# The opening stage of a hybrid decoder block: an order written out for four engines, constants loaded later, query and key blocks per pair of token blocks

## The chip, the cores and the metric

The kernel runs on one core of a Trainium2 chip. The metric is the device time of one execution in microseconds, the median of three runs; lower is better. Engines are named as in the profile: PE is TensorE, DVE is VectorE, ACT is ScalarE, POOL is GpSimd, SP is the queue that only issues transfers. ACT issues transfers too (ACTq).

## The reference

One layer of a decoder block on x of 1024 tokens by 1024 channels, in float32. What matters here is its beginning:

```
u = rms_norm(h, mix_pre_g)                       # h = x
z = einsum('bsd,de->bse', u, w_in)               # 1024 -> 4096 columns
p, q, k, v, gate_a, gate_b = split(z)            # 512 each for p, q, k, v; 1024 for each gate
ya = pool_mixer(p, ...) @ w_branch_a             # windows 2, 4, 8, 16; divided by min(t+1, window)
yb = diff_attention(q, k, v, lambda, ...) @ w_branch_b     # 4 heads, each with two softmaxes
m  = sigmoid(gate_a) * ya + sigmoid(gate_b) * yb
h  = h + rms_norm(m @ w_out, mix_post_g)         # then a SwiGLU feed-forward with its own norms
```
lambda comes from four vectors of 64 numbers: exp(sum(lam_q1 * lam_k1)) - exp(sum(lam_q2 * lam_k2)) + 0.2.

## The kernel before

Precision: each float32 operand of a product is held as a high part `hi` (rounded to the matmul format fp32r by an ACT copy) and a low part `lo` (the difference, by a DVE subtraction), and each product is three matmuls, hi·hi, hi·lo and lo·hi, accumulated in PSUM (`mac`, `triple`).

The big products run as Strassen-like units: `seven_steps` forms the products of two column blocks of weights with both halves of the tokens from seven instead of eight quarter products. Its moving operands are the dictionary `U`: A11, A12, A21, A22 (the normed, transposed x: first index is the half of the tokens, 512 each, second the half of the channels) and four sums S1 to S4 of them; its stationary operands `W` are B11, B21, B22 and T1 to T4, made by `weights` from two raw weight blocks. The sums need the whole of x, so they aren't there at first. Therefore the query and key blocks of heads 0 and 1 (`firsts`, four features of 128 columns) are computed directly from A11 to A22 by `common`, while x still comes in, and the first unit (head 2) starts with line 232 when they are done.

The opening stage, lines 285 to 429, handles x in eight blocks of 128 tokens (`tb`). For each block: load (`load_x`, L304), sum of squares on ACT (`square`, L129), mean on DVE (L124) and its power -1/2 on POOL (L125), scaling by that and by the gain vector g1 on DVE (`normed`, L350), eight transposes of 128x128 on PE into one PSUM tile `x_t` of two banks (L381), high parts on ACT (L385), low parts on DVE (L87), both read from PSUM. For the first four blocks a raw copy goes to `traws` by ACT (L401); for the last four ACT copies half of it (L404) and DVE forms the sums from it and from PSUM (L161). There are two such PSUM tiles, so the transposes of a block wait until the block two before has been read by ACT and DVE. The four weight blocks are loaded by `first_raw` (L207), their high parts taken by ACT (L329) and their low parts by POOL, in four parts each (L334).

Head 0's q and k are computed in pairs of token blocks (`first_pair`, 256 columns a matmul) from block 3 on; head 1's q and k come after, with 512 columns a matmul. `qk_done` splits a finished half of q or k into high and low parts (ACT, then DVE) and sends it to DRAM through the ACT queue (L316).

The order of ACT, DVE and POOL within the loop is as written (`tc.manual_schedule`), but instructions from outside the loop may be put between them; the order of PE and of the transfers is the scheduler's. It put the constants' loads (psc, sgc and four lambda vectors, L432 to L436) at the head of the ACT queue, the scaling of sgc (L446) before the first square, the counts for the pooling windows (iota on POOL, minimum and reciprocal on DVE, L448 to L451) before the first norm, and parts of head 2's and head 3's weight sums (`wf_t`, L161) between the blocks' instructions.

Buffers: 16 of kind `a8` (8 KB a partition: U, traws) and 14 of kind `b4` (4 KB: x blocks, g1, first weights, W, `qk_st`); PSUM tiles `mm`, `fil` (one bank) and `pair` (two banks), two of each.

Of the kernel before, what the change touches and what calls it, by code (L numbers as in the profile page):

```python
# [10 lines left out]
F32 = mybir.dt.float32  # L11
F32R = mybir.dt.float32r
AF = mybir.ActivationFunctionType
ALU = mybir.AluOpType
# [25 lines left out]
def block_kernel(ctx, tc, x, w_in, pool_mix, pool_scale, w_branch_a, lam_q1, lam_k1, lam_q2,  # L40
# [78 lines left out]
    cnt = cp.tile([P, 4, 16], F32, name="cnt")  # L119

# [89 lines left out]
    def weights(first, second):  # L210

        W = {}

        def operand(a, *names):
            for _ in weight_operand(W, a, *names):
                pass

        g, u = raw_weights(first, "wraw"), raw_weights(second, "whi")
        operand(g, "B11", "B21")
        t13, t24 = (wp.tile([P, 2, 4, P], F32, tag="wlo", bufs=2, name=name("wf_t")) for _ in range(2))  # L220
        tt(t13[:, 0], u[:, 0], g[:, 0], ALU.subtract)
# [5 lines left out]
        operand(u[:, 1:], "B22")  # L227
        return W

# [77 lines left out]
    def qk_done(h, e, t, src, st=None):  # L307
# [8 lines left out]
        nc.scalar.dma_start(qkd[h][e][:, :, half(t)], f32(st))  # L316
# [14 lines left out]
    def first_lo(i, part):  # L331
        raw, hi, lo = plain[firsts[i]]
        k = slice(2 * part, 2 * part + 2)
        nc.gpsimd.tensor_tensor(out=lo[:, k], in0=raw[:, k], in1=f32(hi[:, k]), op=ALU.subtract)  # L334

    def common(h, e, t, o, c):
# [15 lines left out]
    for tb in range(2):  # L352
        xts.append(load_x(tb))
    nc.sync.dma_start(g1, mix_pre_g.partition_broadcast(P))
    xts.append(load_x(2))
    first_raw(0)
    first_raw(1)
    for tb in range(3, 5):
        xts.append(load_x(tb))
    with tc.manual_schedule(engines={nc.scalar.engine, nc.vector.engine, nc.gpsimd.engine}):  # L360
        for tb in range(2):
            square(tb)
            rstd(tb)
        for tb in range(2):
            normed(tb)
        first_hi(0)
        for part in range(4):
            first_lo(0, part)
        square(2)
        rstd(2)  # L370
        o = [(fil("q"), fil("k")), (mm("q"), mm("k"))]

        def first_pair(i):
            for e in range(2):
                common(0, e, i // 2, o[i // 2][e], slice(i % 2 * 2 * P, (i % 2 + 1) * 2 * P))

        for tb in range(NB):
            t, cols = tb // 4, slice(tb % 4 * P, (tb % 4 + 1) * P)
            both = pair("x_t")
            for k in range(KD):  # L380
                nc.tensor.transpose(both[:, k // 4, k % 4 * P:(k % 4 + 1) * P], xts[tb][:, k * P:(k + 1) * P], ident)  # L381
            v = [both[:, kq, :].rearrange("p (k t) -> p k t", k=4) for kq in range(2)]
            ops = [[a[:, :, cols] for a in U[f"A{t + 1}{kq + 1}"]] for kq in range(2)]
            for kq in range(2):
                nc.scalar.copy(ops[kq][0], v[kq])  # L385
            if tb + 3 < NB:
                square(tb + 3)
            if tb in (0, 2, 4):
                first_hi(tb // 2 + 1)
            for kq in range(2):  # L390
                sub(ops[kq][1], v[kq], ops[kq][0])
            if tb + 2 < NB:
                normed(tb + 2)
            if tb + 3 < NB:
                rstd(tb + 3)
            if tb < 6:
                for part in range(2):
                    first_lo(tb // 2 + 1, part + tb % 2 * 2)
            if t == 0:
                for kq in range(2):  # L400
                    nc.scalar.copy(traws[f"A1{kq + 1}"][:, :, cols], v[kq])  # L401
            else:
                s1, s2, s3, s4 = (traws[f"S{i + 1}"][:, :, cols] for i in range(4))
                nc.scalar.copy(s1, v[0])  # L404
                tt(s1, v[1], s1, ALU.add)
                tt(s2, s1, s2, ALU.subtract)
                tt(s3, v[1], s2, ALU.subtract)
                tt(s4, s4, s2, ALU.subtract)
            if tb + 5 < NB:
                xts.append(load_x(tb + 5))  # L410
            if tb < 2:
                first_raw(tb + 2)
            if tb in (3, 5, 7):
                first_pair(tb // 2 - 1)
            if tb == 7:
                for e in range(2):
                    qk_done(0, e, 0, o[0][e])
    first_pair(3)
    for e in range(2):
        qk_done(0, e, 1, o[1][e])  # L420
    W = weights(w_cols(o_q, 2), w_cols(o_k, 2))
    for t in range(2):
        o = (fil("q"), fil("k")) if t == 0 else (mm("q"), mm("k"))
        for e in range(2):
            common(1, e, t, o[e], slice(0, HALF))
            qk_done(1, e, t, o[e])
    for n in ("S1", "S2", "S3", "S4"):
        U[n] = operand(n)
        split(U[n], traws[n])


    nc.scalar.dma_start(psc, pool_scale.rearrange("(g p) -> p g", p=P))  # L432
    nc.scalar.dma_start(sgc, subln_g.rearrange("(p o) -> p o", o=1))
    lamt = temp("sg").rearrange("p (i d) -> p i d", d=HD)
    for i, t in enumerate(lams):
        nc.scalar.dma_start(lamt[:, i, :], t.partition_broadcast(P))  # L436
    lsum, lexp, nlam = small(2, "lsum"), small(2, "lexp"), cp.tile([P, 1], F32, name="nlam")
    for i in range(2):
        nc.vector.tensor_tensor_reduce(out=lamt[:, 4, :], in0=lamt[:, 2 * i, :], in1=lamt[:, 2 * i + 1, :],
                                       scale=1.0, scalar=0.0, op0=ALU.mult, op1=ALU.add,  # L440
                                       accum_out=lsum[:, i:i + 1])
    nc.scalar.activation(lexp, lsum, AF.Exp)

    nc.vector.tensor_tensor(out=nlam, in0=lexp[:, 1:2], in1=lexp[:, 0:1], op=ALU.subtract)
    nc.vector.tensor_scalar(nlam, nlam, -LAMBDA_INIT, None, op0=ALU.add)
    nc.scalar.mul(sgc, sgc, 1.0 - LAMBDA_INIT)  # L446
    for g, w in enumerate(WINDOWS):
        nc.gpsimd.iota(cnt[:, g, :], pattern=[[1, 16]], base=1, channel_multiplier=0,  # L448
                       allow_small_or_imprecise_dtypes=True)
        nc.vector.tensor_scalar(cnt[:, g, :], cnt[:, g, :], float(w), None, op0=ALU.min)  # L450
    nc.vector.reciprocal(cnt, cnt)  # L451

    later = []

# [710 lines left out]
```

## Time and profile before

| what | value |
|---|---|
| median of three runs | 1292.57 us (1290.82 to 1293.42) |
| the profiled execution | 1293.83 us, of which the span is 1292.0 us |
| mean granted clock of PE in it | 0.995 |
| instructions | 15663 |
| PE busy | 1248.5 us, 97% of the span |
| DVE, ACT, POOL busy | 836.6, 581.8, 139.0 us |
| first transposes of x | start at 12.00 us |
| first matmul of the first query block | 21.38 us |
| first matmul of the first unit (head 2) | 81.48 us |

Times within the profile are counted from the start of the span. In a timeline row the first two numbers are the start and how long the row lasted, `x8` says that eight like instructions in a row are merged, and the bracket gives the engine's idle time before it and what ended it. In a table of groups, "busy, mean ns of one" are followed by idle time and its releasers. Matmuls are pipelined: what one costs in a stream is the distance between two starts, not the duration in its row.

### The profile page before, as it was taken

What the parts mean: (1) busy time and instruction counts of PE and PEld (TensorE: products, weight loads), DVE (VectorE), ACT (ScalarE), POOL (GpSimd) and SP (SyncE); (2) the same over time, 40 slices, a digit from 0 to 9 for tenths busy, and PEclk for the clock granted to TensorE, in tenths of its full rate; (3) what the DMA queues carried; (4) which work ended last, traced back from release to release, by engine and by line L of the source; (5) the groups of instructions that cost most, each with busy time, mean ns of one, the idle gap of its engine ahead of it and who ended that gap; (6) DMA issues with size and microseconds to landing.
All of it is one profiled execution on the core that took longest, in us unless ns stands there. A gap on an engine that the chain in (4) does not pass through costs nothing.

```text
span 1292.0 us, 15663 instructions
## 1 busy us (share of the span) xinstructions
PE 1248.5 (97%) x5856; PEld 1038.3 (80%) x5856; DVE 836.6 (65%) x1303; ACT 581.8 (45%) x1033; POOL 139.0 (11%) x129
## 2 busy tenths in 40 slices
PE   4899999999989999999999999999999999999997
PEld 4788778888778887878878888888888888888886
DVE  4866685454369988655599565565566538865666
ACT  6444335344486666244564333333333334444542
POOL 3100000000101001001102111111110111000221
PEclk9899999999999999999999999999999999999999
DMA  7245246432598421543333323233223258733235
GB/s 248 66 159 183 100 152 197 131 118 86 173 307 221 139 73 43 168 160 131 112 106 114 105 91 101 96 122 123 86 86 114 98 197 307 242 101 91 89 107 203
DMA packets 139788, 179.16 MB, mean 139 GB/s; under 512 B 8000, under 2 KB 94528, under 8 KB 137280
## 3 DMA queue, kind: packets, MB, share of 16 engines
q1 hardware_dynamic: 127776, 146.56, 36.0%
q10 hardware_dynamic: 11936, 31.60, 6.3%
q8 instruction: 46, 0.75, 0.2%
q14 instruction: 30, 0.25, 0.1%
HBM read 124.39 MB, written 53.74 MB: 138 GB/s over the span
## 4 chain that ended last, share of the span: by engine, by line
PE 82%; DVE 7%; ACT 4%; DMA 3%; issue 2%; POOL 1%; ACTq 0%; SPq 0%; DVEq 0%; POOLq 0%
PE Y L232 9%; PE Y L233 9%; PE Y L234 9%; PE X L232 5%; PE X L233 5%; PE X L234 5%; PE Yd L233 3%; PE Yd L234 3%; PE Yd L232 3%; PE Z L233 2%; PE Z L234 2%; PE Z L232 2%; PE wo L818 2%; PE wo L819 2%; PE wo L817 2%
## 5 line engine op out<-in xcount | busy, mean ns | idle before, releaser
L161 DVE TENSOR_TENSOR p<-Z,p 128x512 f32<-128x512 f32 x35 | 24.2, 691 | 158.4 <-PE Z L234 158.4
L233 PE MATMUL Y<-A_lo,Wh 128*128 128x512 f32 x296 | 115.7, 391 | 0.3 <-DVE A_lo L87 0.3
L232 PE MATMUL Y<-A_hi,Wh 128*128 128x512 f32 x296 | 115.3, 390 | 0.0
L234 PE MATMUL Y<-A_hi,Wl 128*128 128x512 f32 x296 | 115.1, 389 | 0.0
L232 PE MATMUL Y<-S_hi,Wh 128*128 128x512 f32 x280 | 109.2, 390 | 0.0
L232 PE MATMUL X<-S_hi,Wh 128*128 128x512 f32 x280 | 109.1, 389 | 0.1
L233 PE MATMUL Y<-S_lo,Wh 128*128 128x512 f32 x280 | 109.1, 390 | 0.0
L234 PE MATMUL Y<-S_hi,Wl 128*128 128x512 f32 x280 | 109.1, 390 | 0.0
L234 PE MATMUL X<-S_hi,Wl 128*128 128x512 f32 x280 | 109.0, 389 | 0.0
L233 PE MATMUL X<-S_lo,Wh 128*128 128x512 f32 x280 | 109.0, 389 | 0.0
L201 ACT CAST Wh<-wf_t 128x1024 fp32r<-128x1024 f32 x70 | 72.8, 1053 | 69.2 <-PE X L233 30.7
L87 DVE TENSOR_TENSOR w_op<-wd,w_op 128x512 fp32r<-128x512 f32 x77 | 56.4, 732 | 55.2 <-ACT w_op L165 55.2
L87 DVE TENSOR_TENSOR Wl<-wf_t,Wh 128x1024 fp32r<-128x1024 f32 x70 | 86.6, 1244 | 4.6 <-ACT Wh L201 4.6
L201 ACT CAST Wh<-w_raw 128x1024 fp32r<-128x1024 f32 x72 | 60.6, 843 | 63.1 <-PE Z L233 41.9
L165 ACT CAST w_op<-wd 128x512 fp32r<-128x512 f32 x77 | 47.9, 622 | 89.1 <-PE Yd L234 34.4
L87 DVE TENSOR_TENSOR Wl<-w_raw,Wh 128x1024 fp32r<-128x1024 f32 x72 | 69.6, 966 | 14.5 <-ACT Wh L201 14.5
L233 PE MATMUL Yd<-w_op,s_op 128*128 128x512 f32 x176 | 68.7, 390 | 0.2 <-DVE w_op L87 0.2
L232 PE MATMUL Yd<-w_op,s_op 128*128 128x512 f32 x176 | 68.6, 390 | 0.0
L234 PE MATMUL Yd<-w_op,s_op 128*128 128x512 f32 x176 | 68.3, 389 | 0.0
L161 DVE TENSOR_TENSOR wf_t<-w_raw,wf_t 128x512 f32<-128x512 f32 x70 | 65.7, 938 | 1.0
L233 PEld LDWEIGHTS Y<-A_lo,Wh 128*128 128x128 f32 x296 | 55.6, 188 | 11.9 <-DVE A_lo L87 0.7
L232 PEld LDWEIGHTS Y<-A_hi,Wh 128*128 128x128 f32 x296 | 55.6, 188 | 11.6
(259 smaller groups left out, 3050.5 us busy)
## 6 DMA issues: line engine op xcount, KB each, us to landing
s_raw<-fsd SPq DMA_DIRECT2D x35, 512.0 KB, 3.7
w_raw<-in_w_in_dram SPq DMA_DIRECT2D x32, 512.0 KB, 4.0
w_raw<-in_w_ffn_gate_dram SPq DMA_DIRECT2D x22, 512.0 KB, 3.6
w_raw<-in_w_ffn_up_dram SPq DMA_DIRECT2D x22, 512.0 KB, 3.7
fsd<-fss SPq DMA_DIRECT2D x11, 1024.0 KB, 3.8
wd<-in_w_ffn_down_dram SPq DMA_DIRECT2D x44, 256.0 KB, 5.1
fsd<-F SPq DMA_DIRECT2D x33, 256.0 KB, 2.2
qkd<-qk_st ACTq DMA_DIRECT2D x16, 512.0 KB, 3.5
```

The costliest lines, as they stand in the source:

```text
L87: nc.vector.tensor_tensor(out=o, in0=a, in1=f32(hi), op=ALU.subtract)
L161: nc.vector.tensor_tensor(out=o, in0=a, in1=b, op=op)
L165: nc.scalar.copy(hi, a)
L201: nc.scalar.copy(hi, a)
L232: nc.tensor.matmul(o, ah, bh, start=start, stop=False, skip_group_check=goes_on)
L233: nc.tensor.matmul(o, ah, bl, start=False, stop=False, skip_group_check=goes_on)
L234: nc.tensor.matmul(o, al, bh, start=False, stop=stop, skip_group_check=goes_on)
L817: nc.tensor.matmul(o[e], mh[:, k, :], wh, start=k == 0, stop=False)
L818: nc.tensor.matmul(o[e], mh[:, k, :], wl, start=False, stop=False)
L819: nc.tensor.matmul(o[e], ml[:, k, :], wh, start=False, stop=k == KD - 1)
```

## The change

All of it is in the opening stage and in what was hoisted into it.

- The order of PE, ACT, DVE and POOL is written out, instruction by instruction, from the first square to the last sum operand; the weight steps for head 2 (`weights_steps`, the old `weights` cut by yields) and the stores of q and k are placed in it. The issue of a store's transfer (`post`) is placed some instructions behind its conversion.
- The loads of x, g1 and the first weights are issued in another order, and the constants' loads and the iota stand after block 7's copies. The exponential, lambda, sgc and counts come after the units of heads 2 and 3.
- All four first features are computed in pairs of token blocks (`feature(f, p)`), 256 columns a matmul; for the first pair all eight hi·hi matmuls come first, then hi·lo, then lo·hi (`by_pass`).
- ACT takes a high part and a raw copy of every block (`take`); low parts from block 2 on (`take_lo`) and the sums (`take_sums`) read the raw copy in SBUF, not PSUM.
- The low parts of the first weights are taken by DVE, one instruction for each block, not by POOL in four.

```diff
@@ weights
-    def weights(first, second):
-        W = {}
+    def weights_steps(W, first, second):
...
         g, u = raw_weights(first, "wraw"), raw_weights(second, "whi")
+        yield
         operand(g, "B11", "B21")
...
+        yield
         operand(t13, "T1", "T3")
...
+        yield
         operand(t24, "T2", "T4")
+        yield
         operand(u[:, 1:], "B22")
@@ qk_done
-        nc.scalar.dma_start(qkd[h][e][:, :, half(t)], f32(st))
+        if post is None:
+            nc.scalar.dma_start(qkd[h][e][:, :, half(t)], f32(st))
+        else:
+            post.append(lambda: nc.scalar.dma_start(qkd[h][e][:, :, half(t)], f32(st)))
@@ first weights
-    def first_lo(i, part):
+    def first_lo(i):
         raw, hi, lo = plain[firsts[i]]
-        k = slice(2 * part, 2 * part + 2)
-        nc.gpsimd.tensor_tensor(out=lo[:, k], in0=raw[:, k], in1=f32(hi[:, k]), op=ALU.subtract)
+        sub(lo, raw, hi)
@@ common
+        if by_pass:
+            for i, (w, a) in enumerate(((hi, 0), (hi, 1), (lo, 0))):
+                for k in range(KD):
+                    nc.tensor.matmul(o[:, c], w[:, k, :], U[f"A{t + 1}{k // 4 + 1}"][a][:, k % 4, c],
+                                     start=i == 0 and k == 0, stop=i == 2 and k == KD - 1)
+            return
@@ loads: before x0 x1 g1 x2 w0 w1 x3 x4, then x5 w2 x6 w3 x7 in the loop
+    xts.append(load_x(0))
+    xts.append(load_x(1))
     nc.sync.dma_start(g1, mix_pre_g.partition_broadcast(P))
+    first_raw(0)
     xts.append(load_x(2))
+    xts.append(load_x(3))
     first_raw(1)
+    first_raw(2)
+    xts.append(load_x(4))
+    first_raw(3)
@@ the steps (the loop over tb, first_pair and what followed up to L451 are taken out)
+    def turn(tb):
+        both = pair("x_t")
+        for k in range(KD):
+            nc.tensor.transpose(both[:, k // 4, k % 4 * P:(k % 4 + 1) * P], xts[tb][:, k * P:(k + 1) * P], ident)
+        turned[tb] = [both[:, kq, :].rearrange("p (k t) -> p k t", k=4) for kq in range(2)]
+        if tb + 5 < NB:
+            xts.append(load_x(tb + 5))
+    def raw_cols(tb, kq):
+        return traws[(("A11", "A12"), ("S1", "S3"))[tb // 4][kq]][:, :, token_cols(tb)]
+    def take(tb):
+        for kq in range(2):
+            nc.scalar.copy(U[f"A{tb // 4 + 1}{kq + 1}"][0][:, :, token_cols(tb)], turned[tb][kq])
+            nc.scalar.copy(raw_cols(tb, kq), turned[tb][kq])
+    def take_lo(tb):
+        for kq in range(2):
+            hi, lo = (a[:, :, token_cols(tb)] for a in U[f"A{tb // 4 + 1}{kq + 1}"])
+            sub(lo, turned[tb][kq] if tb < 2 else raw_cols(tb, kq), hi)
+    def take_sums(tb):
+        s1, s2, s3, s4 = (traws[f"S{i + 1}"][:, :, token_cols(tb)] for i in range(4))
+        tt(s1, s3, s1, ALU.add)
+        tt(s2, s1, s2, ALU.subtract)
+        tt(s3, s3, s2, ALU.subtract)
+        tt(s4, s4, s2, ALU.subtract)
+    def feature(f, p):
+        if p % 2 == 0:
+            outs[f] = (fil if f < 2 else mm)("qk")
+        common(*firsts[f], p // 2, outs[f], slice(p % 2 * 2 * P, (p % 2 + 1) * 2 * P), p == 0)
+    def constants():
+        # psc, sgc and the four lambda vectors by nc.scalar.dma_start, four iota
...
+    with tc.manual_schedule(engines={nc.tensor.engine, nc.scalar.engine, nc.vector.engine, nc.gpsimd.engine}):
+        # one call a line in the source; "stat" is square and rstd
+        stat(0); stat(1); normed(0); turn(0); normed(1); turn(1); first_hi(0); take_hi(0); take_hi(1)
+        first_lo(0); take_lo(0); take_lo(1); stat(2); normed(2); take_raw(0); feature(0, 0)
+        first_hi(1); first_lo(1); take_raw(1); turn(2); stat(3); first_hi(2); normed(3); first_lo(2)
+        feature(1, 0); take(2); stat(4); take_lo(2); turn(3); normed(4); first_hi(3); feature(2, 0)
+        first_lo(3); take(3); stat(5); take_lo(3); turn(4); normed(5); take(4); stat(6); take_lo(4)
+        take_sums(4); feature(3, 0); turn(5); take(5); normed(6); take_lo(5); stat(7); feature(0, 1)
+        normed(7); take_sums(5); feature(1, 1); turn(6); store(0, 0); take(6); take_lo(6); take_sums(6)
+        post(); store(1, 0); next(wsteps); feature(2, 1); turn(7); take(7); constants(); take_lo(7)
+        post(); store(2, 0); take_sums(7); feature(3, 1); post(); store(3, 0); next(wsteps); post()
+        sum_operand("S1"); feature(0, 2); feature(1, 2); next(wsteps); feature(2, 2); sum_operand("S2")
+        # two reduces for lambda
+        feature(3, 2); feature(0, 3); store(0, 1); next(wsteps); post(); feature(1, 3); store(1, 1)
+        sum_operand("S3"); post(); feature(2, 3); store(2, 1); next(wsteps, None); post()
+        feature(3, 3); store(3, 1); sum_operand("S4"); post()
@@ after the units of heads 2 and 3
+    nc.scalar.activation(lexp, lsum, AF.Exp)
+    # nlam, sgc, minimum of cnt for each window, reciprocal of cnt, as before
```

More of the change, by code (lines that the diff above doesn't have):

```diff
@@ L119, in block_kernel @@
     cnt = cp.tile([P, 4, 16], F32, name="cnt")
+    nlam = cp.tile([P, 1], F32, name="nlam")
     def rstd_of(ss, n, width):
@@ L418, in block_kernel @@
[L418 to L450, printed above, removed]
@@ L451, in block_kernel, with stat @@
-    nc.vector.reciprocal(cnt, cnt)
+    first_raw(2)
+    xts.append(load_x(4))
+    first_raw(3)
+    turned = {}
+    def stat(tb):
+        square(tb)
+        rstd(tb)
+    def turn(tb):
[5 more added lines that the diff above has]
+            xts.append(load_x(tb + 5))
```

201 lines of the change are left out of this document (139 added, 62 removed).

## The prediction

> **What bounds the kernel now.** I read the page's first lines first, then busy time by stretches of the span, then the waits of the opening stretch, and last the timeline of each engine there. TensorE is busy 97% of the span, so a change must either take work from it or fill its pauses. The table of stretches says where they are.
>
> ```profile
> PE 1248.5 (97%) x5856; PEld 1038.3 (80%) x5856; DVE 836.6 (65%) x1303; ACT 581.8 (45%) x1033; POOL 139.0 (11%) x129
> ```
> ```profile
> 0.00:12.00 12.00, 0.00 (x0) 0.03 (x1) 2.65 (x10) 3.67 (x6) 2.19 (x12) 1.00 0.74 214
> 12.00:24.00 12.00, 7.89 (x39) 7.49 (x40) 6.39 (x10) 10.10 (x18) 5.91 (x10) 1.00 1.06 357
> 24.00:37.80 13.80, 12.98 (x109) 12.61 (x107) 8.34 (x14) 10.66 (x20) 7.93 (x13) 1.00 0.39 123
> 37.80:60.00 22.20, 16.67 (x113) 16.24 (x113) 21.23 (x35) 9.20 (x14) 0.61 (x1) 0.85 0.15 48
> 60.00:81.48 21.48, 21.48 (x96) 17.77 (x95) 16.16 (x17) 9.24 (x10) 0.00 (x0) 1.00 0.58 196
> ```
> ```profile
> 82.00:200.00 118.00, 116.91 (x525) 95.10 (x524) 77.73 (x109) 47.36 (x68) 0.00 (x0) 1.00 0.40 140
> ```
> The columns after the stretch and its length are busy time and (instructions) of TensorE, its weight loads, VectorE, ScalarE and GpSimd, then granted clock, DMA share and GB/s. Up to 60 us TensorE is idle 12.0 + 4.1 + 0.8 + 5.5 = 22.4 us, half of all its idle time (1292.0 - 1248.5 = 43.5 us). From 60 on it has no pause, and from 82 to 200 only 1.1 us. So whatever time the first product of the first Strassen-like unit (L232) gains is passed on to the end. It starts at 81.48 now:
>
> ```profile
> 81.48 0.39 PE L232 MATMUL Y<-A_hi,Wh 128*128 128x512 f32 x1
> ```
> What the pauses after the first 12 us wait for (us in total, times, longest), and one wait of the SP queue:
>
> ```profile
> PE x_t L381 <- ACT A_raw L401: 4.1, 1, 4.1
> PE x_t L381 <- DVE S_raw L161: 3.1, 1, 3.1
> PE q L107 <- DVE A_lo L87: 2.2, 1, 2.2
> DVE wf_t L161 <- DMA w_raw<-in_w_in_dram: 2.2, 1, 2.2
> SPq L354 <- DMA psc<-in_pool_scale_dram: 3.6, 1, 3.6
> ```
> Two stand on vector work in the wrong order. At 37.8 VectorE sits 2.2 us for a weight that a hoisted instruction wants, so the sums that free a PSUM tile come late and TensorE sits 3.1 us; at 50.4 the last low parts are 2.2 us late. And the load of g1 waits 3.6 us in the SP queue for a small constant.
>
> **The floor of TensorE's work.** Starts of successive matmuls, slow and fast, at 256 and 512 columns:
>
> ```profile
> 23.02 0.40 PE L107 MATMUL q<-A_lo,w_hi 128*128 128x256 f32 x1
> 23.23 0.30 PE L108 MATMUL q<-A_hi,w_lo 128*128 128x256 f32 x1
> 23.37 1.04 PE L381 MATMUL x_t<-ident,xt 128*128 128x128 f32 x8
> 24.16 0.36 PE L106 MATMUL q<-A_hi,w_hi 128*128 128x256 f32 x1
> 25.08 0.28 PE L107 MATMUL q<-A_lo,w_hi 128*128 128x256 f32 x1
> 25.19 0.28 PE L108 MATMUL q<-A_hi,w_lo 128*128 128x256 f32 x1
> 81.03 0.39 PE L107 MATMUL k<-A_lo,w_hi 128*128 128x512 f32 x1
> 81.26 0.39 PE L108 MATMUL k<-A_hi,w_lo 128*128 128x512 f32 x1
> ```
> 256 columns take 0.12 us fast and 0.21 slow, 512 take 0.227, eight transposes 0.79. Before, there are 192 of 256 and 96 of 512: 23.0 + 21.8 us. After, all 16 blocks have 24 of 256: 384 x 0.12 = 46.1, so splitting head 1's four blocks costs 1.3 us. With 8 x 0.79 = 6.3 of transposes the floor is 52.4 us from the first transpose on.
>
> **The start.** These rows set the first transpose now:
>
> ```profile
> 0.74 0.86 SPq L304 DMA_DIRECT2D xt<-in_x_dram  x2
> 5.24 0.33 SPq L354 DMA_DIRECT2D g<-in_mix_pre_g_dram  x1
> 6.69 0.20 ACT L446 ACTIVATE sgc<-sgc 128x1 f32<-128x1 f32 x1 [1.50 <-DMA sgc<-in_subln_g_dram]
> 6.80 1.04 ACT L129 ACTIVATE junk<-xt 128x1024 bf16<-128x1024 f32 x1
> 8.20 0.55 POOL L125 TENSOR_TENSOR rstd<-ms,mhalf 128x1 f32<-128x1 f32 x1 [6.83 <-DVE cnt L450]
> 10.57 2.48 DVE L350 SCALAR_TENSOR_TENSOR xt<-xt,rstd,g 128x1024 f32<-128x1024 f32 x2 [0.73 <-DMA g<-in_mix_pre_g_dram]
> 12.00 3.64 PE L381 MATMUL x_t<-ident,xt 128*128 128x128 f32 x16 [12.00 <-DVE xt L350]
> ```
> ```profile
> xt<-in_x_dram SPq DMA_DIRECT2D x1, 512.0 KB, 3.8
> ```
> ```profile
> g<-in_mix_pre_g_dram SPq DMA_DIRECT2D x1, 512.0 KB, 5.3
> ```
> g1 lands at 10.5. With six constant loads out of the ScalarE queue and sgc's scaling gone from its head, the first square starts when block 0 lands, 0.74 + 3.8 = 4.5, not at 6.8; its rstd is there 2.0 us later at the latest (6.80 to 8.75 now), at 6.5 to 6.7. g1 is issued third, at about 1.6. It can land no earlier than 1.6 + 3.8 = 5.4, and at the worst at 10.5 as now, if the slot in the queue was not what kept it. I take 7.6: three pieces in a row at 357 GB/s (the 12:24 row; 1.47 us each) behind block 0. So the first norm ends at 8.9 and transposes start at 9.0: 3.0 us gained, between 0 and 4.5. The pieces behind follow at 1.5 us (w0 9.1, x2 10.6, x3 12.1, w1 13.6, w2 15.1, x4 16.6, w3 18.1); each microsecond by which all from g1 on are late moves the first unit by one.
>
> **The new order, walked through.** The order is now written out for four engines, so I went through it instruction by instruction, each starting when its engine and its inputs are free, 0.07 us after the releaser, with the durations of the rows above and of these (mean ns of one):
>
> ```profile
> L87 DVE TENSOR_TENSOR A_lo<-x_t,A_hi 128x512 fp32r<-128x512 f32 x16 | 10.3, 684 | 6.4 <-ACT A_hi L385 6.4
> L334 POOL TENSOR_TENSOR w_lo<-w_raw,w_hi 128x256 fp32r<-128x256 f32 x16 | 11.3, 735 | 4.0 <-ACT w_hi L329 4.0
> L87 DVE TENSOR_TENSOR Wl<-w_raw,Wh 128x1024 fp32r<-128x1024 f32 x1 | 1.2, 1215 | 0.0
> L87 DVE TENSOR_TENSOR S_lo<-S_raw,S_hi 128x2048 fp32r<-128x2048 f32 x2 | 4.6, 2283 | 0.0
> L385 ACT CAST A_hi<-x_t 128x512 fp32r<-128x512 f32 x16 | 8.7, 602 | 0.1
> ```
> (Each overlaps the next of its engine by some 0.1 us.) VectorE takes over the four weight subtractions from GpSimd, 4 x 1.2 = 4.9 us for 11.3 us there. Its sum over the stage: norms 8 x 1.2, first weights 4.8, low parts 16 x 0.6, sums 16 x 0.6, stores 8 x 0.6, W of head 2 6.6, S operands 4 x 2.2, small ones 1.5, together 55 us. Up to the low part of block 7 it is 33 us, and that ends at 48 with all waits, while TensorE reaches the first block that needs it at 57. ScalarE gets four more raw copies (2.4 us), which free the PSUM tile without VectorE; reading PSUM or SBUF costs VectorE the same here. The constants' six issues, about 0.5 us each, now stand in ScalarE's queue behind block 7's copies (at 41): behind them wait a store and its successors, which hold up no operand, so I cost them at nothing, at most 3 us if a PSUM tile of q or k is then wanted. The deferred cnt and lambda operations come before their first reader and beside units in which VectorE is idle a third of the time: nothing. Ordering the first block by passes lets 8 matmuls start before the low parts: 0.4 us either way.
>
> TensorE's pauses after 9.0 in this walk: 1.6 us for the high parts of block 1 (the first matmul at 13.8), 0.7 at 50 for head 1's q tile to be stored, and 2.1 at the first unit, whose PSUM tile waits for a store queued on VectorE behind S3. That is 4.4. To it comes the slow clock:
>
> ```profile
> 52.60 0.39 PE L107 MATMUL q<-A_lo,w_hi 128*128 128x256 f32 x1 [2.23 <-DVE A_lo L87]
> 54.25 0.42 PE L107 MATMUL q<-A_lo,w_hi 128*128 128x256 f32 x1
> 54.46 0.41 PE L108 MATMUL q<-A_hi,w_lo 128*128 128x256 f32 x1
> 57.43 0.28 PE L108 MATMUL k<-A_hi,w_lo 128*128 128x256 f32 x1
> 57.55 0.28 PE L106 MATMUL k<-A_hi,w_hi 128*128 128x256 f32 x1
> ```
> Work was still slow at 23.0 after transposes from 12.0, and a 2.2 us pause brought 0.21 us back from 54.0 to 57.4, 16 matmuls x 0.09 = 1.5 us lost. A slow transpose costs 0.1 us more (16 in 3.64 us, against eight in 0.79): 1.6 us for two blocks. If full speed comes one such stretch after the first matmul, at 17.5, 18 matmuls add 1.7, together 3.3 us; if at 20, 30 add 2.8, together 4.4. I take the later.
>
> Sum: 9.0 + 52.4 + 4.4 + 4.4 = 70.2, the walk itself 70.4, against 81.48: 11.1 us gained. Its operands are there (B11 at 55, S1 59, S2 63, S3 70, S4 76, wanted at 70, 73, 76, 81 and 84), so nothing waits behind it. The profiled execution took 1293.8 beside a span of 1292.0, 1.3 us above the median of three. 1293.8 - 11.1 = 1282.7; against the median, 1281.5. I say 1282.
>
> By the row at 54.25 the 2.1 us pause at the first unit could bring another slow stretch, 1.5 us, and 1283.5; I leave that to the range, since the pauses of 0.8 and 0.2 us brought none. [...]
>
> Transposes from 12.0 to 15.6 left the matmuls at 23.0 slow, so I do not let the transposes at 9.0 count towards the clock; if they did, the walk would give 68.9, and 1280. [...]
>
> **The rivals.** Loads late: g1 and all behind it 3 us later than I put them, since nothing shows that the queue slot alone kept g1 back, or every piece at 2 us. The walk then gives a first unit at 73.4, and with both and the pauses doubled 77: 1284.5 to 1288. For it: g1 took 5.3 us to land against 3.8. Against: the mean of 214 GB/s in the first 12 us against 357 in the next leaves room.
>
> Given back: the stage ends 11 us early and a later wait takes it back, head 3's weights or the k and v stores first. The 82:200 row speaks against it, with 1.1 us idle in 118. 1290 to 1295.
>
> Slower: the written order on TensorE lets no later work fill a pause, so pauses over 2 us recur and the slow clock stays on. A slow matmul costs 0.093 us more; to be 2.6 us above the time before, the 11.1 and 2.6 more must go, 13.7 us, which is 147 of the 384 matmuls, or nine slow stretches of 16 beyond the first. From there on it decides. The walk has one pause over 2 us, and the kernel before had one slow stretch for its pause of 2.2 and one for that of 3.1. 1295 to 1300.
>
> More gained: g1 lands at 5.4, so transposes start at 7.9 (the rstd is the later input), the clock is up early, and the pauses shrink to 2 us: 7.9 + 52.4 + 2 + 2 = 64.3, a gain of 17 and 1275.5; half of that way is 1278.
>
> **How the numbers follow.** My forecast (gain 8 to 14, 1278.5 to 1284.5) has 0.64, loads late 0.15, more gained 0.07, given back 0.08, slower 0.06. 0.2% is 2.6 us, about what a measurement of this kernel can tell from no change; faster by more is 0.64 + 0.15 + 0.07 = 0.86. The range 1277 to 1288 leaves out half of "more gained" and the two last cases.
>
> **What would show it.** g1's norm ending near 9 and the first transposes there (now 12.0); the first L232 matmul near 70; TensorE idle in the first 70 us some 13 us; GpSimd without L334; no wait on A_raw or S_raw over 1 us; 82:200 unchanged. I am wrong if g1 still lands after 10, if the clock stays low past 25, or if x5 to x7 stand in the SP queue behind a weight until after 31, when their squares are due.

## The result, and the profile after

The changed kernel takes 1280.34 us (median of four runs, 1279.42 to 1284.72) against 1292.83 us of the kernel before on the same chip: a ratio of 0.9913, 95% interval 0.9899 to 0.9927, so 12.5 us less. Run again later (f2 below) it took 1281.12 us, ratio 0.9924 [0.9906, 0.9943]. The profiled execution took 1280.2 us with a span of 1278.3 us, 13.7 us below the span of before; granted clock 0.999.

The first page line of busy time, and the table of stretches cut as in the prediction (busy us and instructions of TensorE, weight loads, VectorE, ScalarE, GpSimd; then clock, DMA share, GB/s):

```profile
PE 1246.2 (97%) x5952; PEld 1039.0 (81%) x5952; DVE 839.4 (66%) x1307; ACT 583.0 (46%) x1037; POOL 129.5 (10%) x113
```
```profile
0.00:12.00 12.00, 3.01 (x14) 3.01 (x15) 3.98 (x6) 5.63 (x8) 1.80 (x8) 1.00 0.80 278
12.00:24.00 12.00, 11.32 (x80) 10.92 (x79) 9.01 (x15) 11.37 (x22) 2.03 (x3) 1.00 1.10 377
24.00:37.80 13.80, 13.80 (x118) 13.63 (x117) 12.30 (x19) 9.93 (x21) 2.77 (x7) 1.00 0.28 79
37.80:60.00 22.20, 21.07 (x174) 20.66 (x173) 19.60 (x32) 11.03 (x16) 0.00 (x0) 1.00 0.29 102
82.00:200.00 118.00, 116.89 (x527) 95.08 (x526) 83.98 (x121) 45.67 (x66) 0.00 (x0) 1.00 0.43 152
```
Up to 60 us TensorE is idle 9.0 + 0.7 + 0 + 1.1 = 10.8 us, where it was 22.4 before, and the clock of the fourth stretch is 1.00 instead of 0.85. The stretch 82:200 has the same 1.1 us of idle time, so the gain is passed on. All waits of TensorE up to 82 us (total, times, longest):

```profile
PE x_t L389 <- DVE xt L367: 9.0, 1, 9.0
PE qk L106 <- DVE qk_st L322: 1.0, 1, 1.0
PE qk L352 <- ACT A_hi L402: 0.7, 1, 0.7
```
The waits on A_raw, S_raw and A_lo are gone. The timeline of the start, of TensorE's first block, of its pause at 50 and of the first unit:

```profile
7.65 2.48 DVE L367 SCALAR_TENSOR_TENSOR xt<-xt,rstd,g 128x1024 f32<-128x1024 f32 x2 [0.58 <-DMA g<-in_mix_pre_g_dram]
8.99 3.68 PE L389 MATMUL x_t<-ident,xt 128*128 128x128 f32 x16 [8.99 <-DVE xt L367]
13.34 2.08 PE L352 MATMUL qk<-A_hi,w_hi 128*128 128x256 f32 x8 [0.68 <-ACT A_hi L402]
15.22 1.91 PE L352 MATMUL qk<-A_lo,w_hi 128*128 128x256 f32 x8
16.92 1.20 PE L352 MATMUL qk<-A_hi,w_lo 128*128 128x256 f32 x8
17.96 1.03 PE L389 MATMUL x_t<-ident,xt 128*128 128x128 f32 x8
18.75 1.20 PE L352 MATMUL qk<-A_hi,w_hi 128*128 128x256 f32 x8
21.71 1.04 PE L389 MATMUL x_t<-ident,xt 128*128 128x128 f32 x8
50.43 0.39 PE L106 MATMUL qk<-A_hi,w_hi 128*128 128x256 f32 x1 [1.02 <-DVE qk_st L322]
68.17 0.40 PE L241 MATMUL X<-S_hi,Wh 128*128 128x512 f32 x1
```
The first transposes stand at 8.99 (12.00 before), the first unit's first product at 68.17 (81.48 before). Before and changed kernel, each from 0 to its first unit:

```profile
0.00:81.48 81.48, 59.02 (x352) 54.14 (x353) 54.76 (x83) 42.88 (x66) 16.64 (x34) 0.96 0.52 170
```
```profile
0.00:68.17 68.17, 57.37 (x448) 56.40 (x449) 53.03 (x82) 41.95 (x68) 6.61 (x18) 1.00 0.53 180
```
The account of these 13.3 us: from 0 to its first unit the kernel before has TensorE busy for 59.0 us, 7.9 above its floor of 51.1 (23.0 + 21.8 + 6.3); the changed one is busy for 57.4, 5.0 above its floor of 52.4. So 11.7 us come from idle time and 2.9 from time above the floor, less 1.3 for splitting head 1. Most of the 2.9 is clock: behind its pauses the kernel before has two stretches of 3.4 us at half of full clock (0.50, the third number from the end), and the changed kernel has no such stretch before its first unit:

```profile
40.33:43.73 3.40, 2.82 (x14) 2.85 (x15) 3.40 (x6) 1.14 (x3) 0.00 (x0) 0.50 0.45 134
53.98:57.39 3.41, 3.41 (x18) 3.41 (x17) 3.34 (x6) 3.15 (x3) 0.00 (x0) 0.50 0.02 5
```

Four starts follow the gain through the run: first transposes of x, first product of the first unit, first transpose of the values (vT, behind the units of heads 2 and 3), and the span. Later stages vary by some us from run to run, so vT is the mark for the opening stage and the time for the whole. Transposes to span are those of the one traced execution, the median is that of all. All in us:

| kernel | transposes | first unit | vT | span | median | ratio to before |
|---|---|---|---|---|---|---|
| before | 12.00 | 81.48 | 131.5 | 1292.0 | 1292.83 | 1 |
| changed | 8.99 | 68.17 | 118.6 | 1278.3 | 1280.34 | 0.9913 [0.9899, 0.9927] |
| f2, the changed kernel again | 8.8 | 68.00 | 118.4 | 1279.1 | 1281.12 | 0.9924 [0.9906, 0.9943] |
| e1 | 11.84 | 69.65 | 119.7 | 1283.2 | 1283.70 | 0.9926 [0.9909, 0.9943] |
| e2 | 8.91 | 75.99 | 126.0 | 1285.6 | 1288.83 | 0.9973 [0.9963, 0.9983] |
| e3 | 8.9 | 72.99 | 123.0 | 1285.8 | 1286.80 | 0.9951 [0.9935, 0.9966] |
| e4 | 8.8 | 70.18 | 120.5 | 1281.2 | 1283.52 | 0.9928 [0.9905, 0.9951] |
| e5 | 9.0 | 66.95 | 117.3 | 1278.9 | 1280.52 | 0.9903 [0.9882, 0.9925] |
| e6 | 8.92 | 70.17 | 120.5 | 1286.4 | 1282.95 | 0.9932 [0.9909, 0.9954] |
| e8 | 8.96 | 66.37 | 120.4 | 1284.1 | 1285.93 | 0.9939 [0.9919, 0.9959] |
| e9 | 17.80 | 76.34 | 126.7 | 1285.6 | 1288.98 | 0.9969 [0.9959, 0.9979] |
| e10 | 8.80 | 66.44 | 116.5 | 1277.6 | 1280.97 | 0.9904 [0.9884, 0.9925] |
| f1 | 8.88 | 66.53 | 116.6 | 1280.9 | 1280.57 | 0.9905 [0.9889, 0.9921] |
| f3 | 10.38 | 68.06 | 118.1 | 1278.4 | 1281.11 | 0.9914 [0.99, 0.9928] |

The kernel before measured 1292.24 beside e1, e2, e3 and e8, 1293.12 beside e4, e5, e9 and e10, and 1292.56 beside e6 and f1 to f3.

Part of what varies behind vT is the clock. Leaving out the one at the very end of every run, the traces have such stretches of 3.4 us at half clock behind vT: none in changed, f2, f3, e2, e9 and e10, one in before, e1, e4 and e5, two in e3, e8 and f1, three in e6. From vT to the end it takes 1158.9 to 1161.1 us with none, 1160.6 to 1163.5 with one, 1162.8 to 1164.3 with two and 1165.9 with three. So where a time differs by more than vT does, part of it can be the clock of that execution and not the edit.

### The profile page after: what moved, and what is told of

The parts are those of the page before. It is cut to its first block, busy times and chain, and to the rows that moved or that the text cites. A ratio compares the mean times of both kernels' runs of the same rounds, so it can differ in the third digit from the quotient of the medians.

```text
span 1278.3 us, 15840 instructions
## 1 busy us (share of the span) xinstructions
PE 1246.2 (97%) x5952; PEld 1039.0 (81%) x5952; DVE 839.4 (66%) x1307; ACT 583.0 (46%) x1037; POOL 129.5 (10%) x113
## 4 chain that ended last, share of the span: by engine, by line
PE 79%; DVE 7%; ACT 5%; DMA 4%; issue 4%; POOL 1%; ACTq 0%; SPq 0%; DVEq 0%; POOLq 0%
PE Y L241 9%; PE Y L242 9%; PE Y L243 9%; PE X L241 5%; PE X L242 5%; PE X L243 5%; PE Yd L242 3%; PE Yd L243 3%; PE Yd L241 3%; PE Z L242 2%; PE Z L243 2%; PE Z L241 2%; PE o L776 2%; PE wo L934 2%; PE wo L935 2%
```

## The experiments

The theory: the gain is a sum of an earlier start, of an order in which nothing TensorE wants stands behind work that is not yet due, and of head 1's pairs filling what pauses remain. The rival reading: most of it is one thing, either the constants, or the clock.

**e1, the constants at the head again.**

```diff
+    constants()
+    nc.scalar.mul(sgc, sgc, 1.0 - LAMBDA_INIT)
     xts.append(load_x(0))
@@ the written order
         take(7)
-        constants()
         take_lo(7)
```


> The changed kernel with the six constant loads and the scaling of sgc at the head of the ACT queue again, as before the change; everything else stays. Theory (g1 waits in the SP queue behind the first constant, and every stage behind the first norm follows it): first transposes at 12.0 us instead of 9.0, first product of the first unit 3 us later than 68.2, at 71.2, and 3 us slower, about 1283.5. Rival (the early start is swallowed by the pauses of the stage, so that only the order on TensorE counts): first transposes at 12.0 but the first unit within 1 us of 68.2, about 1280.5.

The transposes came at 11.84, 2.85 us later, as expected, but the first unit only 1.5 us later. The waits of TensorE show why: the pause at 50 is not there.

```profile
PE x_t L403 <- DVE xt L367: 11.8, 1, 11.8
PE qk L352 <- ACT A_hi L416: 0.7, 1, 0.7
```
So the late place of the constants has a price of its own. In e10 (below) they are neither at the head nor in the middle of ScalarE's queue, and against it e1's unit is 3.2 us later (69.65 against 66.44): the late start shifts everything by its full size. The start is worth 3.2 us, of which the changed kernel gives back 1.7. The time rose by 3.4 us (2.6 against f2), of which only 1.2 stand at vT; one stretch at half clock, at 556.9 us of the trace, is among the rest.

**e2, the kernel before with the constants late, and nothing else.**

```diff
                     qk_done(0, e, 0, o[0][e])
+                nc.scalar.dma_start(psc, pool_scale.rearrange("(g p) -> p g", p=P))
+                nc.scalar.dma_start(sgc, subln_g.rearrange("(p o) -> p o", o=1))
...
```


> The kernel before, with the constants' loads and the iota placed behind block 7's copies, where the change has them; nothing else is changed. Theory (the start is one part of several): first transposes near 9, but the x blocks still stand behind weight loads in the SP queue and head 1's products still come last, so the first unit starts 1 to 3 us before 81.5 and the time is 1290 to 1292. Rival (the constants carry the whole gain): first unit near 70, about 1281. Second rival (the pauses swallow it): within 0.5 us of before.

The transposes came at 8.91 and the first unit at 75.99, 5.5 us earlier: more than the 1 to 3 us expected and less than the rival's 11 (a unit near 70). The waits of the old order are still there:

```profile
PE x_t L381 <- ACT A_raw L401: 4.2, 1, 4.2
PE x_t L381 <- DVE S_raw L161: 2.9, 1, 2.9
PE q L107 <- DVE A_lo L87: 2.0, 1, 2.0
```
Of the 2.4 us above the start's 3.1, some 1.8 lie in the clock, granted 0.98 and 0.84 in 20:41 and 41:60 before, and 0.92 and 1.00 in e2 (21 x 0.02 + 19 x 0.16 = 3.5 us of full speed missing, against 21 x 0.08 = 1.7): of the two stretches at half clock one is gone. The 0.8 us that TensorE waits for a mean (ms) in the kernel before is gone too. The constants' place alone therefore gives 5.5 of the 13.3 us at the first unit, and the other edits together the rest. (It is not quite the place of the change: behind block 7 the issues start at 58.73 here, at 42.57 in the changed kernel.)

**e3, head 1 at 512 columns in four blocks, as before.**

```diff
     def feature(f, p):
+        if f >= 2:
+            outs[f] = mm("qk")
+            common(*firsts[f], p // 2, outs[f], slice(0, HALF), False)
+            return
...
-        feature(2, 0)
         first_lo(3)
```
(In the order, head 1's block for a half of the tokens stands where its second pair stood.)

> The changed kernel with head 1's query and key blocks computed as before the change, 512 columns at a time: the two blocks of the first half where their second pair of token blocks stood, the two of the second half at the end. TensorE has 1.3 us less work by the row distances (0.227 against two of 0.12). Theory (the pairs of head 1 fill pauses between the transposes): pauses of 2 to 3 us before the transposes of blocks 4 and 5, some of them followed by the slow clock, and a first unit 3 to 5 us later, at 71 to 73: 1283 to 1285. Rival (the split only costs): first unit 1.3 us earlier, about 1279.

The first unit came 4.8 us later, in the expected range. The four pauses of TensorE on the normed x (15.5 us, the start's 8.9 among them, against 9.0 in one) are those that head 1's pairs fill. The two long ones:

```profile
25.36 1.06 PE L389 MATMUL x_t<-ident,xt 128*128 128x128 f32 x8 [3.31 <-DVE xt L367]
29.28 1.94 PE L389 MATMUL x_t<-ident,xt 128*128 128x128 f32 x8 [2.87 <-DVE xt L367]
```
The eight transposes of the last row took 1.94 us, against 1.06 in the row above it, and the granted clock of 20:41 is 0.84, against 1.00 in the changed kernel: behind the 3.31 and 2.87 us of idle time TensorE was slow too. The time rose by 6.5 us, of which 4.5 stand at vT.

**e8, the constants behind the last operand.**

```diff
         take(7)
-        constants()
         take_lo(7)
...
         sum_operand("S4")
         post()
+        constants()
```
(The two reduces for lambda go with them.)

> The changed kernel with the six constant loads, the iota and the two reductions for lambda behind the last step of the written order. Theory (their issues, 42.6 to 48.4 us in the ACT queue, delay the store of head 1's first query half and with it TensorE by the 1.0 us pause at 50.4): the pause goes, first unit 1 to 1.8 us earlier, at 66.5 to 67.2, about 1279. Rival (another store or low part is late instead): the pause stays within 0.3 us, no change.

The pause at 50 went and the unit came at 66.37, 1.8 us earlier, as expected. But the time rose to 1285.93, and vT came 1.8 us later: the price had moved. ScalarE's timeline (ACTq rows are transfers issued by its queue) and TensorE's waits, up to 82 us:

```profile
70.87 0.80 ACTq L450 DMA_DIRECT2D psc<-in_pool_scale_dram  x1
...
74.46 0.44 ACTq L453 DMA_DIRECT2D sg<-in_lam_k_dram  x1
74.94 0.58 ACT L277 COPY p<-Y 128x512 f32<-128x512 f32 x1 [3.58 <-PE Z L243]
```
```profile
PE Y L241 <- ACT u L283: 1.4, 1, 1.4
PE Y L241 <- ACT p L277: 0.9, 1, 0.9
```
The copies that free the first unit's PSUM tiles stand behind 4 us of issues, and a third wait of 0.9 us on VectorE follows before vT. At both places what costs is the block of issues in the queue of an engine that computes. Of the 5.6 us in the time 1.8 stand at vT; the traced execution, which is the median one, has two stretches at half clock behind it.

**e10, the constants on the SP queue, behind the last first weight.**

```diff
     first_raw(3)
+    constants()          # all six by nc.sync.dma_start
...
         take(7)
-        constants()
         take_lo(7)
```
(sgc is scaled behind the two reduces.)

> The changed kernel with the six constant loads issued from the SP queue behind the last of the first weights, the iota at the start, and the scaling of sgc behind the lambda reductions. Theory (the issues cost ACT its queue wherever they stand in it: 1.0 us of TensorE at 50, or 3.2 us when they meet the first unit's evictions): no ACT wait of 4.4 us at 49, no TensorE pause at 50.4, first unit 1 to 1.8 us earlier than 68.2, first transposes of the values 1 to 1.8 us before 118.6, and 1278.5 to 1279.3. Rival (the loads behind them, x5 to x7, come late instead): waits of the squares on x blocks, first unit at 68.2 or later.

No stall, no pause at 50; first unit at 66.44, vT 116.5, 1.7 and 2.1 us earlier, and the squares did not wait. The time, 1280.97, does not show it: two runs of the changed kernel differ by 0.8 us, and the interval is 0.4% wide.

**e4, the first weights' low parts on GpSimd, four a block.**

```diff
     def first_lo(i):
         raw, hi, lo = plain[firsts[i]]
-        sub(lo, raw, hi)
+        for part in range(4):
+            k = slice(2 * part, 2 * part + 2)
+            nc.gpsimd.tensor_tensor(out=lo[:, k], in0=raw[:, k], in1=f32(hi[:, k]), op=ALU.subtract)
```


> The changed kernel with the low parts of the four first weight blocks on POOL again, in four parts each (0.735 us a part). Theory (the low part is wanted only as the last of the three passes, and VectorE is nearly full from 20 to 60 us): VectorE gets 4.9 us back, POOL's 2.8 us a block come just in time, and the first unit starts 0 to 2 us earlier than at 68.2; 1278.5 to 1281. Rival (the move off POOL was part of the gain, because POOL's work slows VectorE or stands ahead of the rstd): first unit 1 us later or more, 1281.5 to 1284.

The theory, that VectorE would be relieved and the unit come 0 to 2 us earlier, fell; it came 2.0 us later. GpSimd and VectorE in e4:

```profile
18.55 0.15 DVE L125 TENSOR_SCALAR ms<-ss 128x1 f32<-128x1 f32 x1 [1.68 <-ACT junk L130]
19.52 0.55 POOL L126 TENSOR_TENSOR rstd<-ms,mhalf 128x1 f32<-128x1 f32 x1
20.04 4.25 POOL L347 TENSOR_TENSOR w_lo<-w_raw,w_hi 128x256 fp32r<-128x256 f32 x4
20.10 1.75 DVE L369 SCALAR_TENSOR_TENSOR xt<-xt,rstd,g 128x1024 f32<-128x1024 f32 x1 [1.39 <-POOL rstd L126]
```
The mean is ready at 18.70, its rstd starts at 19.52, when the four parts ahead of it are through; this norm, beside the next four, also takes 1.75 us, as the one of the next block does, where the others take 1.28. So part of the gain of moving them is that GpSimd has nothing before the rstd, and part may be that VectorE is not slowed beside it; no run separates the two.

**e5, low parts and sums from PSUM again.**

```diff
-            nc.scalar.copy(raw_cols(tb, kq), turned[tb][kq])
+            if tb < 4 or kq == 0:
+                nc.scalar.copy(raw_cols(tb, kq), turned[tb][kq])
...
-            sub(lo, turned[tb][kq] if tb < 2 else raw_cols(tb, kq), hi)
+            sub(lo, turned[tb][kq], hi)
...
-        tt(s1, s3, s1, ALU.add)
+        tt(s1, turned[tb][1], s1, ALU.add)
```


> The changed kernel with low parts and sums read from PSUM as before the change, and ACT's second raw copy of the last four blocks left out. Theory (the norm of block n+2 stands behind the low part of block n on VectorE anyway, so holding the PSUM tile longer costs nothing, and ACT has four copies of 0.6 us less): first unit within 0.5 us of 68.2 or up to 1 us earlier, 1279.3 to 1280.8. Rival (freeing the PSUM tile early is what lets the transposes run ahead): waits of transposes on A_lo or S_raw return, 2 us or more in sum, 1282.3 or more.

The waits for VectorE did not come back (0.2 us on S_raw), and the unit came 1.2 us earlier, with the pause at 50 gone: ScalarE has four copies less. VectorE's mean durations for the low parts, first of the changed kernel, then of e5:

```profile
L87 DVE TENSOR_TENSOR A_lo<-S_raw,A_hi 128x512 fp32r<-128x512 f32 x8 | 5.1, 681 | 0.0
```
```profile
L87 DVE TENSOR_TENSOR A_lo<-x_t,A_hi 128x512 fp32r<-128x512 f32 x16 | 10.3, 682 | 0.4 <-ACT A_hi L402 0.4
```
Reading SBUF is no faster, and freeing the PSUM tile sooner was worth nothing in this order. "Sums from SBUF" is no source of the gain.

**e6, the first pair without passes.**

```diff
-        common(*firsts[f], p // 2, outs[f], slice(p % 2 * 2 * P, (p % 2 + 1) * 2 * P), p == 0)
+        common(*firsts[f], p // 2, outs[f], slice(p % 2 * 2 * P, (p % 2 + 1) * 2 * P), False)
```


> The changed kernel with the first pair of token blocks computed in the order of all others, high and low by turns, not by passes. Theory (from 13 to 41 us ACT and VectorE bind the stage, TensorE has slack there): the first matmul waits for the low parts, at 15 instead of 13.3, and the first unit starts 0 to 1 us later; 1280.3 to 1281.5. Rival (the walk by which the time was forecast: TensorE binds from its first matmul on): first unit 3 us later, 1283.5.

The first block: the second matmul waits for the low part, and the block is through at 19.56 instead of 17.96.

```profile
13.27 0.58 PE L106 MATMUL qk<-A_hi,w_hi 128*128 128x256 f32 x1 [0.68 <-ACT A_hi L402]
14.49 0.58 PE L107 MATMUL qk<-A_lo,w_hi 128*128 128x256 f32 x1 [0.64 <-DVE A_lo L87]
...
19.35 0.41 PE L108 MATMUL qk<-A_hi,w_lo 128*128 128x256 f32 x1
19.56 1.41 PE L389 MATMUL x_t<-ident,xt 128*128 128x128 f32 x8
```
All 24 matmuls ran at the slow distance of 0.21, where the last eight of the changed kernel were fast; with the wait of 0.64 this makes most of the 1.6 us, and the unit is 2.0 later, between the two expectations. How much is the wait and how much the moment at which the clock rose in this run (see the end) is open. The median rose by 2.6 us, not resolved against f2.

**e9, 72 matmuls of 128 columns ahead of the first transposes**, written to a PSUM tile that nobody reads, to bring the clock up.

```diff
+        hot = cp.tile([P, P], F32R, name="hot")
+        nc.scalar.copy(hot, ident)
+        for i in range(2):
+            hp = pair("hot")
+            for j in range(36):
+                nc.tensor.matmul(hp[:, j % 2, :P], hot, hot, start=True, stop=True)
         stat(0)
```


> The changed kernel with 72 matmuls of 128 columns on a rounded identity on TensorE, whose results nothing reads, ahead of the first transposes, from about 2.3 us on, while x still comes in. Theory (the slow clock at the start is a matter of what TensorE did just before): the 16 first transposes take 1.8 us instead of 3.7 and the first 16 matmuls 0.12 instead of 0.21 each; as ACT and DVE bind part of the stage from 13 to 41, the first unit starts 1 us earlier, at 67.2, and the time is about 1279. Rival (nothing ahead of real work counts, or the extra matmuls end after 9.0): first transposes as slow or later, 1280 to 1282.

The theory fell twice over. Each took 0.21 us, so they ran to 17.8 and delayed the transposes by 8.8 us; and after 15 us of them the transposes began as slow as ever (four in 1.07 us, against seven in 0.97 two us later):

```profile
2.38 15.62 PE L464 MATMUL hot<-hot 128*128 128x128 f32 x72 [2.38 <-ACT hot L460]
17.80 1.07 PE L389 MATMUL x_t<-ident,xt 128*128 128x128 f32 x4
19.74 0.97 PE L389 MATMUL x_t<-ident,xt 128*128 128x128 f32 x7
```

**f1, e10 and e5 together; f3, f1 with g1's load ahead of block 1's.** f2 is the changed kernel again, with no edit, to see how far two runs of it lie apart.

```diff
     xts.append(load_x(0))
-    xts.append(load_x(1))
     nc.sync.dma_start(g1, mix_pre_g.partition_broadcast(P))
+    xts.append(load_x(1))
```


> The changed kernel with the constants on the SP queue and with low parts and sums read from PSUM, without the second raw copy of the last four blocks. Theory (the constants' 1.7 us go; the raw copies that go were 1.3 us of the same pause): first unit at 66 to 66.5, values at 116 to 116.6, some 2 us faster than the changed kernel, 1278.5. Rival (the two gains add, because they sit at different places): first unit at 65.2, values at 115.2, 1277.5.

> The changed kernel itself, for comparison on the same chip. All theories: first unit at 68.2, first transposes of the values at 118.6 within 1 us, about 1280.5.

> As the run with constants on SP and sums from PSUM, and with g1 issued ahead of the second x block. Theory (g1's landing at 7.5 is what the first norm waits for, the rstd is there at 6.4): first transposes at 8.0 to 8.3 instead of 8.9, the first unit 0.5 to 0.8 us earlier. Rival (the second block, now landing later, holds the stage instead): first transposes earlier, first unit unchanged within 0.3 us.

f1: the unit at 66.53 and vT at 116.6 are those of e10. The two edits remove one and the same pause, so their gains do not add. Its 2 us at vT do not reach the time (1280.57). Later in the traced execution, at 1282.73 the slowest of the four, TensorE waits 3.1 us for a query tile from DRAM, where the changed kernel waits 1.0. First f1, then the changed kernel, between 200 and 540 us:

```profile
PE s L736 <- DMA QB<-qkd: 3.1, 1, 3.1
```
```profile
PE s L735 <- DMA QB<-qkd: 1.0, 1, 1.0
```
Around the end of that wait, and once more at 428.9, f1's clock stands at half for 3.4 us, where the changed kernel has 1.00:

```profile
336.75:340.16 3.41, 3.03 (x7) 2.48 (x8) 1.23 (x2) 0.09 (x1) 0.00 (x0) 0.50 0.98 376
428.91:432.31 3.40, 3.40 (x12) 3.40 (x13) 3.28 (x9) 1.02 (x4) 0.00 (x0) 0.50 0.09 14
```
e6, with a unit 2 us later than the changed kernel's, had 3.0 there, so the wait does not follow the earlier start; its cause is not settled.

f3: the transposes came at 10.38 and not at 8.0 to 8.3. Not the load was at fault, which landed at 1.18 + 5.1 = 6.3:

```profile
6.05 0.56 POOL L126 TENSOR_TENSOR rstd<-ms,mhalf 128x1 f32<-128x1 f32 x1 [4.40 <-DVE cnt L644]
7.74 1.06 ACT L130 ACTIVATE junk<-xt 128x1024 bf16<-128x1024 f32 x1 [1.96 <-DMA xt<-in_x_dram]
8.92 0.15 DVE L125 TENSOR_SCALAR ms<-ss 128x1 f32<-128x1 f32 x1 [2.05 <-ACT junk L130]
9.04 1.28 DVE L367 SCALAR_TENSOR_TENSOR xt<-xt,rstd,g 128x1024 f32<-128x1024 f32 x1
```
The rstd of block 0 is there at 6.6, but the written order has `stat(1)` ahead of `normed(0)`: on VectorE the norm stands behind block 1's mean, and that behind block 1's load, which now lands after g1. A queue in order turned a load moved back into a start moved back. No kernel here beats the changed one in time: e5, e10, f1 and f3 lie between 1280.5 and 1281.1, and differences of 1 us among them are not resolved.

## Why the prediction was right, and where its terms were off

Direction and size held, and so did the main steps of the mechanism: first transposes 9.0 as said (8.99), g1 landing at 7.54 against 7.6, the gain passed on through the units, and a gain at the first unit of 13.3 us against 11.1. The first unit came at 68.2 instead of 70.2, a sum in which errors partly cancel: the floor came out 1.3 us higher, pauses and slow clock 3.3 us lower. By the terms of the sum:

- **The start, 9.0:** right. e1 against e10 puts its worth at 3.2 us, against 3.0.
- **The floor, 52.4:** 1.3 us short. It counted 0.12 us a matmul and nothing for starting again: the 24 matmuls behind a block of transposes take 21.71 - 18.75 = 2.96 us, not 2.88, and matmuls behind transposes or a pause lose this 0.08 in eight places. Blocks that follow each other directly lose nothing: the two from 30.16 on, 48 matmuls, take 5.84 us, 48 x 0.12 and 0.08 once. The other 0.6 are short gaps at 29.2, 49.3 and 53.4, of 0.16 to 0.27 us.
- **The pauses, 4.4:** they were 1.7. Block 1's high parts cost 0.68 and not 1.6. The pause at 50 was 1.02 and not 0.7. The 2.1 us at the first unit did not come: behind the written order the scheduler put a product for the tile X first, which was free, and the one for Y behind it. The walk had not foreseen that, so this part of the better result is luck.
- **The slow clock, 4.4:** it was 3.8. The two blocks of transposes lost 3.67 - 1.58 = 2.1 us (1.6 taken), the first 24 matmuls 4.62 - 2.96 = 1.7 (2.8 taken), since full speed came at 17 and not at 20. The walk's alternative of 17.5 fits this run, but kernels with the same start had full speed anywhere from 13.2 or earlier (e3, e4, e8, f1) to 20.3 (e6; see the end), so the term is a draw and not a constant. Both moments, 17.5 and 20, were the author's estimates; in the kernel before, the only trace there was, full speed came 1.9 us behind the first matmul (23.26 against 21.38). The term's premise, that transposes do not count towards the clock, does not hold in general: in e3, e4, e8 and f1 the first eight matmuls took 1.23 us, against 2.08 in the changed kernel, when only transposes had run. The kernel before left it open: behind its transposes of 12.0 to 15.6 TensorE paused for 4.1 us.
- **The constants' six issues, nothing, at most 3:** wrong choice within its bounds. The reason given, that only a store stands behind them, was true and not enough: that store frees the PSUM tile that head 1 wants.

```profile
42.57 3.30 ACTq L450 DMA_DIRECT2D psc<-in_pool_scale_dram  x1
...
49.05 0.60 ACT L321 ACTIVATE qk_st<-qk 128x512 fp32r<-128x512 f32 x1 [4.40 <-DMA sg<-in_lam_q_dram]
```
  ScalarE computes nothing for 4.4 us, the store ends late and TensorE pauses 1.02 us at 50; without it (e10) the unit is 1.7 earlier.
- **PSUM or SBUF the same:** right for VectorE's durations (e5). That the extra copies cost ScalarE something that matters, 1.2 us at the unit through that same pause, was not seen.
- **By-pass, 0.4 either way:** undersized; e6 gives 2.0 at the unit, with the clock in it.
- **VectorE taking GpSimd's subtractions:** it was costed as load on VectorE only. e4 shows a gain of 2.0 us, in part because GpSimd's queue is then free for the rstd.

What e3 says was not in the sum as a term of its own: head 1's pairs were booked as a cost of 1.3 us, and what they buy, 4.8 us at the unit, was inside the walk. The rivals: loads were not late, nothing was given back in the units, and the slow clock did not recur in the changed kernel, though it did behind vT in other kernels here.

The parts undone one at a time are worth, at vT, 3.2 (start, e1 against e10), 4.5 (pairs, e3), 2.0 (GpSimd, e4) and 2.0 (passes, e6), of 12.9; the constants' place in ScalarE's queue costs 2.1 (e10) and the extra copies 1.2 (e5), both through one pause. They overlap, so they are no account. That the order of ScalarE and VectorE as such took away the 4.2, 2.9 and 2.0 us waits of e2 is argued from those waits having gone, not isolated by a run; whether TensorE's own order, written out, or the new order of the loads brings anything was not tried.

## What to carry to other kernels

In these runs a block of transfers issued from a computing engine's queue held up the work behind it; against the same six in the queue that only issues (e10), they cost this kernel 1.7 us at the first unit and 2.1 at vT from the middle of its first stage (changed kernel), and 3.9 at vT from in front of the first unit (e8), while up to 82 us of e10 TensorE waited for nothing but the first norm (8.8 us) and block 1's high parts (0.7). When an order is written out by hand, go through each in-order queue for what stands ahead of the instruction that starts the chain: the rstd behind weight parts (e4, 2.0 us at the first unit, part of it from this) and the norm behind a later block's mean (f3, 1.5 against f1) each cost about as much as a whole edit was to bring. And splitting a long product into pieces that can start early may be dear in the floor and still pay: 1.3 us more work brought the unit 4.8 us forward.

## What the runs showed of the hardware that was not expected

- **The moment of full clock varied between like runs, and in four it came with nothing but transposes before it.** Matmuls started at 13.1 to 13.4 us in most kernels here. They were near full speed at once in e3, e4, e8 and f1 (the first eight in 1.23 us), from about 17 or 17.5 in the changed kernel, f2, e5 and e10, and only from about 20.3 in e6. In the first four nothing but the transposes, from about 8.9 on, had run on TensorE. e8's first block, against 2.08 us for the same eight matmuls of the changed kernel (the row at 13.34):

```profile
13.18 1.23 PE L352 MATMUL qk<-A_hi,w_hi 128*128 128x256 f32 x8 [0.68 <-ACT A_hi L402]
```
  e8 was 0.9 us ahead of e10 at the third block (21.70 against 22.61) and 0.07 at the first unit (66.37 against 66.44): what a fast start gained it lost again in waits for the norm. The granted clock column says 1.00 at the start of every run, also while matmuls stand 0.21 us apart: the traces have no clock record before the first full speed (23.26 in the kernel before, 17.11 in the changed kernel), and the column counts such time as full. Each stretch at half clock in these traces, but for the one at the end of every run, lasts 3.41 us or, in e3 from 26.75 on, twice that, and in the kernel before the full speed between its first two lasts 10.24 us. The stretch at 53.98 there began 1.4 us behind the end, at 52.60, of a pause of 2.2 us. And of pauses of like size not each had such a stretch behind it: behind the waits for a query tile near 335 us the clock fell in e8 (1.8 us) and not in e10 (2.1 us).
- **72 matmuls of 128 columns, in fp32r, took 0.21 us each** through 15.4 us without a pause (e9), as much as a slow one of 256 columns, and the first four transposes behind them took 1.07 us, against 0.97 for seven two us later. Whether it is the width or the operand, an identity against itself, was not separated.
- **A transfer's issue on ScalarE's queue took 0.44 to 3.3 us** in its row, the 3.3 (at 42.57) for a load of 2 KB; in e8 the same one took 0.80, in the kernel before 0.48. During the 3.3 us ScalarE still ran four copies, until 44.66, so how much of it is the issue itself is open.
